# Second norm of a hybrid decoder layer: where the matmul with ones, the first silu and gate products, and three of the products x*r stand in the queues

## The chip, the cores and the metric

The kernel runs on one core of one Trainium2 chip. A core has four compute engines, each with its own queue of instructions in a fixed order: TensorE (PE in the profile; its weight loads are PEld), VectorE (DVE), ScalarE (ACT) and GpSimd (POOL). SyncE (SP) issues DMAs. An instruction starts when its engine has come to it and when what it waits for has been signalled, so an instruction that waits holds up all that is queued behind it on its engine. The metric is the device time of one execution in microseconds (us), as a median over runs.

## The reference

One layer of a decoder trunk for 512 prompt tokens and 8 sample tokens, all in fp32, with D = 1024 features. The change touches only the border between the attention/recurrent mix and the feed-forward network (FFN):

```python
x = x + g1 * mixed                       # mixed = (...) @ w_o
h2 = rms_norm(x, norm2_g) * (1.0 + sc2) + sh2
gu, up = jnp.split(h2 @ w_ffn_in, 2, axis=-1)      # 1024 -> 2 * 2816
x = x + g2 * ((jax.nn.silu(gu) * up) @ w_ffn_out)  # 2816 -> 1024
```

with `rms_norm(x, g) = x * rsqrt(mean(x*x) + eps) * g` over the features. `sc2`, `sh2` and the gates come from the conditioning and are one value per feature for the prompt, and one per feature and token for the samples. A final norm follows.

## The kernel before, in words

**Layout.** All activations are held transposed: features on the 128 partitions, tokens along the row. `x` is eight tiles of 128 features x 520 tokens (512 prompt tokens, then 8 sample columns). The 520 columns are worked in two halves of 260 (`HALVES`).

**Products.** Each fp32 operand is split in two numbers of a shorter format, a high part (`...h`, `whi`) and a rest (`...l`, `wlo`); a product is three matmuls (high x high, rest-weight x high, high x rest) for each of eight feature tiles, so a *half product* is 24 matmuls of 128x128 by 128x260 (`part_product`, L302 to L309). In each group of three the rest operand `h2l` is used last. Weight splits (a cast on ACT, a subtraction on DVE, L249 and L251) are made a few products ahead, into a ring of three buffers; raw weights come by DMA from SP's queue into a ring of two (`load_chunks`).

**The second norm.** `by_halves("wo", ...)` runs the products with `w_o`, first half of the tokens for all eight feature tiles, then the second half. After each one `residual` adds the result to `x` (DVE), and `sum_squares` squares it on ACT (L399) and adds it to `ss2` on POOL, or on DVE for the last two tiles (L400). `rstd_half` (L402) then sums over the partitions by a matmul with a 128x128 matrix of ones into the bank `r` (L407, plain fp32, two passes in the trace), takes the root on ACT (L408, one table load of its own) and the reciprocal on DVE (L409). `h2_half` (L1435) makes, for each feature tile f, the product x*r (L1446: POOL for the first half, DVE for the second), the high part `h2h` on ACT (L1448), the scaled and shifted value again on ACT or DVE (L1453, L1455), two small products for the 8 sample columns on POOL (L1450, L1451) with a copy of these 8 columns on ACT (L1457), and the rest `h2l` on DVE (L1458). The first half's norm is done inside the `w_o` products (`wo_between`).

**The first two FFN tiles.** The loop at L1640 runs four products (gate and up of two tiles of 128 hidden features) by halves: m = 0 to 3 for the first half of the tokens, then again for the second half. m even is a gate product, followed by `swish` (silu on ACT, L1500); m odd is an up product, followed by `times_up` (silu(gate) * up on DVE, L1504). Between the first half's m = 0 and m = 1 stands the second half's norm, as the second half's x is complete only when the last `w_o` product has been evacuated. Products from the second half need `h2h` and `h2l` of it. PSUM has 8 banks that are handed out in turn.

After that come the tiles 2 and 3 as whole products (`ffn_tile`; `fig`, `fiu` in the trace), and from tile 4 on `fast_tile`, which needs sums and differences of blocks of h2 that POOL makes (`h2_blocks`, L1577).

**What sets the order.** The order of each engine's queue is written at build time: a planner goes through the program with estimated times, takes for each engine what is ready by these estimates, and among ready work what stands first in the code. So the queues need not follow the code line by line. `tc.issue_after(ins)` keeps the instructions traced inside it behind `ins` in the queue of that instruction's engine; it adds no wait between engines.

Of the kernel before, what the change touches and what calls it, by code (L numbers as in the profile page):

```python
# [11 lines left out]
AF = mybir.ActivationFunctionType  # L12
ALU = mybir.AluOpType
# [4 lines left out]
D = 1024  # L18
# [10 lines left out]
HALF = NT // 2  # L29
HALVES = ((0, HALF), (HALF, NT))  # L30
# [35 lines left out]
def kernel(ctx, tc, xT, par, gates, b_f, cst, cse, own, cache_k, cache_v, cache_lf, pt,  # L66
# [3 lines left out]
    pe, act, dve, pool, sp = nc.tensor, nc.scalar, nc.vector, nc.gpsimd, nc.sync  # L70
# [9 lines left out]
    def slot(name, cols=NT, dt=F32, parts=128):  # L80
        return heap.tile([parts, cols], dt, name=name, tag="slot")

    def bank(name, parts=128, cols=512):
        return psp.tile([parts, cols], F32, name=name, tag="bank")
# [9 lines left out]
    x = []  # L94
# [12 lines left out]
    eps = keep.tile([128, 1], F32, name="eps")  # L107
# [76 lines left out]
    state = {"n": 0, "dma": 0, "split": 0, "load": 22, "lead": 11, "due": 0, "age": 1}  # L184
# [19 lines left out]
    def load_chunks(upto):  # L204
        while state["dma"] < len(chunks) and state["dma"] <= upto:
            c = state["dma"]
            if c in joined:
                raw = pgp.tile([128, GROUP, 256], F32, name="wraw", tag="pg")
            else:
                raw = wp.tile([128, KT, 256], F32, name="wraw", tag="wraw", bufs=2)  # L210
            o = 0
            for src, r0, nk, c0, n in chunks[c]:
                sp.dma_start(raw[:, :nk, o:o + n],
                             src[r0:r0 + nk * 128, c0:c0 + n].rearrange("(k p) c -> p k c", p=128))
                o += n
            raws[c] = raw
            state["dma"] += 1
# [70 lines left out]
    def begin(last=None):  # L288
        n = state["n"]
        state["n"] += 1  # L290
        last = len(units) - 1 if last is None else last
        if n < 42:
            tick(KEYS[n], n in VALUES)
        load_chunks(units[reach(n, last, state["load"])][0])
        split_upto(reach(n, last, state["lead"]))
        flush()
        return n

    def half_product(n, j, a, out):
        part_product(n, *HALVES[j], (lambda k: a(k, j)) if callable(a) else a, out)  # L300

    def part_product(n, t0, t1, a, out):  # L302
        hi, lo = splits[n]
        nk = units[n][2]
        for k in range(nk):
            ah, al = a(k) if callable(a) else (v[:, t0:t1] for v in a[k])
            for m, (wt, at) in enumerate(((hi, ah), (lo, ah), (hi, al))):
                state["mm"] = pe.matmul(out[:, :t1 - t0], lhsT=wt[k], rhs=at, start=k == 0 and m == 0,  # L308
                                        stop=k == nk - 1 and m == 2)  # L309

    def run_later(n):
        for fn in later.pop(n, []):
            fn()
# [88 lines left out]
    def rstd_half(name, ssum, r, j, more=()):  # L402
        t0, t1 = HALVES[j]
        ps = bank(f"{name}_{j}")
        parts = [ssum[:, t0:t1], *more]
        for n, q_ in enumerate(parts):
            pe.matmul(ps[:, :HALF], lhsT=ones, rhs=q_, start=n == 0, stop=n == len(parts) - 1)  # L407
        act.activation(r[:, t0:t1], ps[:, :HALF], AF.Sqrt, bias=eps, scale=1.0 / D)  # L408
        dve.reciprocal(r[:, t0:t1], r[:, t0:t1])  # L409

    def amplitude(name, scl, g):
# [125 lines left out]
    for f in range(KT):  # L537
        t = slot("sq1")
# [14 lines left out]
    for f in range(KT):  # L553
        t = slot("xn")
# [10 lines left out]
    for g3 in (0, 3):  # L565
# [10 lines left out]
        for n in range(6):  # L576
            t0, t1 = HALVES[n % 2]
# [317 lines left out]
    ready = []  # L895
    for i in range(KT):
        if i % 4 == 0:
            qtp.append(bank(f"qt{i}", NS))
        if i < 6:
            t = qpart[i]  # L900
            for j, (t0, t1) in enumerate(HALVES):
                b = bank(f"q{i}_{j}")
# [3 lines left out]
        else:  # L906
            t = slot("q")
# [521 lines left out]
    ss2, r2 = slot("ss2"), slot("r2")  # L1429
    h2 = []  # L1430
# [4 lines left out]
    def h2_half(j):  # L1435
        t0, t1 = HALVES[j]
        e_ = min(t1, NP)
        for f in range(KT):
            if j == 0:
                h2.append((slot("h2h", dt=F32R), slot("h2l", dt=F32R)))  # L1440
                if f % 2 == 0:
                    pair = pgp.tile([128, 2, NT], F32, name="h2r", tag="pg")
                    h2raw.extend((pair[:, 0], pair[:, 1]))
            t = h2raw[f]
            hi, lo = h2[f]
            (dve if j else pool).tensor_tensor(t[:, t0:t1], x[f][:, t0:t1], r2[:, t0:t1], ALU.mult)  # L1446
            a_, b_ = amp2[0][:, f], mod[:, 3, f]
            act.activation(hi[:, t0:e_], t[:, t0:e_], AF.Identity, scale=a_[:, 0:1], bias=b_[:, 0:1])  # L1448
            if j:
                pool.tensor_tensor(t[:, NP:], t[:, NP:], a_[:, 1:9], ALU.mult)  # L1450
                pool.tensor_tensor(t[:, NP:], t[:, NP:], b_[:, 1:9], ALU.add)  # L1451
            if j and f in ON_ACT:
                act.activation(t[:, t0:e_], t[:, t0:e_], AF.Identity, scale=a_[:, 0:1], bias=b_[:, 0:1])  # L1453
            else:
                dve.tensor_scalar(t[:, t0:e_], t[:, t0:e_], a_[:, 0:1], b_[:, 0:1], ALU.mult, ALU.add)  # L1455
            if j:
                act.copy(hi[:, NP:], t[:, NP:])  # L1457
            dve.tensor_tensor(lo[:, t0:t1], t[:, t0:t1], hi[:, t0:t1].bitcast(F32), ALU.subtract)  # L1458
# [32 lines left out]
    def wo_between(j):  # L1491
        rstd_half("r2", ss2, r2, j)
        h2_half(j)
# [12 lines left out]
    def last_product(ac):  # L1506
# [40 lines left out]
        for j, (t0, t1) in enumerate(LAST_PARTS):  # L1547
            for i in range(KT):
                if j == 0:
                    begin(u + KT - 1)  # L1550
                b = bank(f"fo{i}_{j}")
                part_product(u + i, t0, t1, ac, b)
                done(i, j, t0, t1, b)
                if j and i == 0:
                    norm(0, *LAST_PARTS[0])
        norm(1, *LAST_PARTS[1])

    def pair_out():
        return slot("ach", dt=F32R), slot("acl", dt=F32R)
# [78 lines left out]
    ac, ts, ready = [], [slot("sw") for _ in range(PLAIN)], []  # L1638
    u = state["n"]
    for j in range(2):  # L1640
        for m in range(2 * PLAIN):
            if j == 0:
                begin(u + 3)
            b = bank(f"fi{m}_{j}")
            half_product(u + m, j, h2, b)
            ready.append((times_up if m % 2 else swish, b, ts[m // 2], j))
            if j == 0 and m == 0:
                rstd_half("r2", ss2, r2, 1)
            if j or m:
                for fn, *args in ready:  # L1650
                    fn(*args)
                ready.clear()
            if j == 0 and m == 0:
                h2_half(1)
            first = u + 2 * PLAIN
            if j == 0:
                load_chunks(units[first + m][0])
            elif m:
                split_upto(first + m - 1)
    for t in ts:  # L1660
        out = pair_out()
# [72 lines left out]
```

## Time and profile before

| what | us |
|---|---|
| runs | 1032.33, 1027.59, 1031.36 |
| median | 1031.36 |
| the profiled execution | 1029.59 |
| its span (first to last instruction) | 1027.9 |
| PE busy | 992.3 (97%) |
| DVE busy | 796.8 (78%) |
| ACT busy | 551.0 (54%) |
| POOL busy | 328.6 (32%) |
| granted TensorE clock, mean | 0.994 |

The times of the trace are counted from the start of the span. In a timeline row stand the start, the duration, the engine, the line of the kernel, the operation, what it writes and reads, and in brackets how long the engine was idle before it and what ended that. Rows of several equal instructions are merged (x4). Matmuls overlap in the pipeline: each is shown with some 0.28 us while they start 0.12 us apart. A row of the waits reads: who waited, for whom, us in total, times, the longest. A row of groups with three numbers gives the shortest, median and longest duration in ns.

The part of the trace that matters runs from 658.8 us, the first FFN matmul, to 685.8 us, the first matmul of tile 2.

### The profile page before, as it was taken

To read this page: it belongs to the slowest core of one execution; us is meant where nothing else is said; L and a number is where in the kernel's file an instruction comes from. 1 tells how busy PE (TensorE), PEld (TensorE's weight loads), DVE (VectorE), ACT (ScalarE), POOL (GpSimd) and SP (SyncE) were. 2 spreads that over 40 slices of the span, in tenths; PEclk is the share of its full clock that TensorE was granted. 3 is DMA by queue.
4 is the path that set the end of the run, shared out by engine and by line. 5 is a ranking of instruction groups with operands and counts; after the bars stand their busy time and mean duration, and the time that the engine had idled before them with its cause. 6 is when DMAs were issued, how large, how long until landed. Compare 5 with 4: busy or idle time off the path is not lost.

```text
span 1027.9 us, 21296 instructions
## 1 busy us (share of the span) xinstructions
PE 992.3 (97%) x7994; PEld 918.8 (89%) x7994; DVE 796.8 (78%) x1423; ACT 551.0 (54%) x1132; POOL 328.6 (32%) x424
## 2 busy tenths in 40 slices
PE   4999999999999999999999999999999999999996
PEld 1788989999898988878888989999999999999996
DVE  5446999998989987886756544878888888888864
ACT  4433665857682267776875233565444444445453
POOL 0214511111133235654430001484432433434212
PEclk9899999999999999999999999999999999999998
DMA  9987987878888999988665784324243342333212
GB/s 323 307 280 285 306 290 217 261 233 276 261 254 310 323 314 306 310 259 274 219 235 185 252 302 126 83 62 115 71 124 99 87 124 72 93 104 103 62 63 84
DMA packets 165419, 206.99 MB, mean 201 GB/s; under 512 B 9906, under 2 KB 126146, under 8 KB 165250
## 3 DMA queue, kind: packets, MB, share of 16 engines
q1 hardware_dynamic: 148594, 152.52, 47.9%
q0 software_dynamic: 13040, 46.67, 13.7%
q10 hardware_dynamic: 3680, 6.42, 1.7%
q8 instruction: 63, 1.03, 0.4%
q14 instruction: 42, 0.34, 0.1%
HBM read 192.49 MB, written 13.09 MB: 200 GB/s over the span
## 4 chain that ended last, share of the span: by engine, by line
PE 70%; DVE 14%; DMA 6%; ACT 5%; issue 3%; SPq 0%; POOL 0%; POOLq 0%; DVEq 0%; ACTq 0%
PE fo L308 12%; PE pb L308 4%; PE gb L308 4%; PE ga L308 3%; PE k L308 3%; PE wo L308 3%; PE v L308 3%; DVE wlo L251 2%; DMA wraw<-in_w_in_dram 2%; PE gr L308 2%; PE xr L308 2%; DVE pg L733 2%; PE qp L530 2%; PE pv L818 2%; PE po L1261 2%
## 5 line engine op out<-in xcount | busy, mean ns | idle before, releaser
L249 ACT CAST whi<-wraw 128x1024 fp32r<-128x1024 f32 (+1 forms) x79 | 82.0, 1039 | 121.2 <-PE pb L308 35.1
L251 DVE TENSOR_TENSOR wlo<-wraw,whi 128x1024 fp32r<-128x1024 f32 (+1 forms) x79 | 101.3, 1284 | 32.6 <-ACT whi L249 30.5
L273 ACT CAST wb<-ws 128x512 fp32r<-128x512 f32 x72 | 44.8, 622 | 91.1 <-PE fo L308 63.6
L308 PE MATMUL fo<-ach,wb 128*128 128x260 f32 x512 | 93.3, 282 | 0.0
L685 POOL DMA_DIRECT2D pg<-in_cache_k_dram x74 | 39.4, 533 | 142.7 <-DVE S L734 70.3
L308 PEld LDWEIGHTS fo<-ach,wb 128*128 128x128 f32 x512 | 78.8, 188 | 0.0
L274 DVE TENSOR_TENSOR wb<-wraw,wb 128x512 fp32r<-128x512 f32 x86 | 74.2, 863 | 5.0 <-ACT wb L273 4.4
L274 DVE TENSOR_TENSOR wb<-ws,wb 128x512 fp32r<-128x512 f32 x72 | 65.8, 913 | 14.0 <-ACT wb L273 12.2
L264 POOL TENSOR_TENSOR ws<-wraw 128x512 f32<-128x512 f32 x18 | 26.6, 1480 | 153.8 <-DMA wraw<-in_w_fi_dram 124.8
L308 PE MATMUL fo<-acl,wb 128*128 128x260 f32 x256 | 72.3, 282 | 0.0
L273 ACT CAST wb<-wraw 128x512 fp32r<-128x512 f32 x86 | 53.6, 623 | 32.7 <-ACT cp L1622 5.8
L733 DVE TENSOR_TENSOR pg<-pg,qb 128x1024 f32<-128x1024 f32 x48 | 58.0, 1227 | 2.5 <-DMA pg<-in_cache_k_dram 2.4
L734 DVE TENSOR_REDUCE S<-pg 128x16 f32<-128x1024 f32 x48 | 57.0, 1207 | 0.1
L1218 POOL TENSOR_SCALAR p<-p,mu 128x128 f32<-128x128 f32 (+3 forms) x28 | 36.4, 1310 | 49.2 <-DVE mu L1214 31.3
L308 PEld LDWEIGHTS fo<-acl,wb 128*128 128x128 f32 x256 | 48.2, 188 | 0.0
L1212 ACT ACTIVATE p<-p,mu 128x128 f32<-128x128 f32 (+3 forms) x64 | 35.3, 553 | 15.9 <-DVE mu L1211 15.6
L308 PE MATMUL v<-hh,whi 128*128 128x260 f32 x128 | 37.3, 291 | 1.1 <-DVE pl L1232 1.1
L308 PE MATMUL pb<-oh,whi 128*128 128x260 f32 x128 | 36.7, 287 | 1.0 <-ACT oh L1319 1.0
L308 PE MATMUL k<-hh,whi 128*128 128x260 f32 x128 | 37.3, 291 | 0.0
L308 PE MATMUL gb<-hh,whi 128*128 128x260 f32 x128 | 37.0, 289 | 0.0
L308 PE MATMUL ga<-hh,wlo 128*128 128x260 f32 x128 | 36.3, 284 | 0.7 <-DVE wlo L251 0.7
L308 PE MATMUL pa<-gl,whi 128*128 128x260 f32 x128 | 36.1, 282 | 0.7 <-DVE gl L342 0.7
(1099 smaller groups left out, 3965.8 us busy)
## 6 DMA issues: line engine op xcount, KB each, us to landing
araw<-in_ada_w_dram SPq DMA_DIRECT2D x48, 512.0 KB, 7.0
wraw<-in_w_fi_dram SPq DMA_DIRECT2D x44, 512.0 KB, 4.7
pg<-in_cache_k_dram POOLq DMA_DIRECT2D x42, 512.0 KB, 6.0
pg<-in_cache_v_dram SPq DMA_DIRECT2D x42, 512.0 KB, 5.1
wraw<-in_w_in_dram SPq DMA_DIRECT2D x34, 512.0 KB, 7.8
wraw<-in_w_in_dram SPq DMA_DIRECT2D x11, 1024.0 KB, 10.0
pg<-in_cache_v_dram POOLq DMA_DIRECT2D x22, 512.0 KB, 6.4
pg<-in_cache_k_dram POOLq DMA_DIRECT2D x32, 256.0 KB, 5.7
```

What stands on the lines that cost most here:

```text
L249: state["act"] = act.copy(hi[:, :k1 - k0], src)
L251: state["last"] = dve.tensor_tensor(lo[:, :k1 - k0], src, hi[:, :k1 - k0].bitcast(F32), ALU.subtract)
L264: pool.tensor_tensor(s1, a21, a22, ALU.add)
L273: state["act"] = act.copy(t[:, :4], src)
L274: state["last"] = dve.tensor_tensor(t[:, 4:], src, t[:, :4].bitcast(F32), ALU.subtract)
L308: state["mm"] = pe.matmul(out[:, :t1 - t0], lhsT=wt[k], rhs=at, start=k == 0 and m == 0, stop=k == nk - 1 and m == 2)
L530: state["mm"] = pe.matmul(b[:, :HALF], lhsT=wt, rhs=at[:, t0:t1], start=k == 0 and m == 0, stop=k == 3 and m == 2)
L685: done.append(eng.dma_start(pg, cache[bass.ds(r, 1), :, c0:c1].rearrange("a p c -> (a p) c")))
L733: dve.tensor_tensor(pg, pg, q, ALU.mult)
L734: last = dve.tensor_reduce(S[r // 2][:, c:c + H], pg.rearrange("p (h d) -> p h d", d=DH), AX.X, ALU.add)
L1212: act.activation(p[:, :n + 128], p[:, :n + 128], AF.Exp, bias=mu[:, 0:1], scale=-1.0, accum_out=mu[:, 1:2])
L1218: (pool.tensor_scalar(p, p, mu[:, 2:3], None, ALU.mult) if a and i + 1 < KT else act.activation(p, p, AF.Copy, scale=mu[:, 2:3]))
```

## The change

Three edits:

1. The matmul with ones for the second half is issued inside the second half product (m = 1, first half of the tokens), after the fourth of its eight feature tiles, through a new argument `mid` of `half_product` and `part_product`. Before, it came after the product m = 0. `h2_half(1)` moves with it, behind the product m = 1.
2. `rstd_half` keeps its root instruction in `state["root"]`; what follows the products (`swish`, `times_up`) is traced inside `issue_after(root)`. The root is on ACT, so the silus are tied; a gate product reads a silu's output and so follows.
3. In the second half of `h2_half` the products x*r of the feature tiles 5, 6 and 7 go to POOL; tiles 0 to 4 stay on DVE.

The code order of `load_chunks` for the next chunk (m = 0) and of `begin` for m = 1 is thereby ahead of the norm's second half. No operation is added or dropped, no size is changed.

```diff
-    def half_product(n, j, a, out):
-        part_product(n, *HALVES[j], (lambda k: a(k, j)) if callable(a) else a, out)
+    def half_product(n, j, a, out, mid=None):
+        part_product(n, *HALVES[j], (lambda k: a(k, j)) if callable(a) else a, out, mid)
 
-    def part_product(n, t0, t1, a, out):
+    def part_product(n, t0, t1, a, out, mid=None):
...
                 state["mm"] = pe.matmul(out[:, :t1 - t0], lhsT=wt[k], rhs=at, start=k == 0 and m == 0,
                                         stop=k == nk - 1 and m == 2)
+            if mid is not None and k == nk // 2 - 1:
+                mid()
...
-        act.activation(r[:, t0:t1], ps[:, :HALF], AF.Sqrt, bias=eps, scale=1.0 / D)
+        state["root"] = act.activation(r[:, t0:t1], ps[:, :HALF], AF.Sqrt, bias=eps, scale=1.0 / D)
         dve.reciprocal(r[:, t0:t1], r[:, t0:t1])
...
-            (dve if j else pool).tensor_tensor(t[:, t0:t1], x[f][:, t0:t1], r2[:, t0:t1], ALU.mult)
+            (dve if j and f < 5 else pool).tensor_tensor(t[:, t0:t1], x[f][:, t0:t1], r2[:, t0:t1], ALU.mult)
...
             b = bank(f"fi{m}_{j}")
-            half_product(u + m, j, h2, b)
+            half_product(u + m, j, h2, b, (lambda: rstd_half("r2", ss2, r2, 1)) if j == 0 and m == 1 else None)
             ready.append((times_up if m % 2 else swish, b, ts[m // 2], j))
-            if j == 0 and m == 0:
-                rstd_half("r2", ss2, r2, 1)
+            if j == 0 and m == 1:
+                h2_half(1)
             if j or m:
-                for fn, *args in ready:
-                    fn(*args)
+                with tc.issue_after(state["root"].ins):
+                    for fn, *args in ready:
+                        fn(*args)
                 ready.clear()
-            if j == 0 and m == 0:
-                h2_half(1)
```

## The prediction

> **What bounds the kernel now.** I read the page first, for the span and the busy shares, then the windows by stage, then TensorE's waits on either side of the change, and at last the order of each engine's instructions in that stage. From the page:
>
> ```profile
> span 1027.9 us, 21296 instructions
> ...
> PE 992.3 (97%) x7994; PEld 918.8 (89%) x7994; DVE 796.8 (78%) x1423; ACT 551.0 (54%) x1132; POOL 328.6 (32%) x424
> ...
> L249 ACT CAST whi<-wraw 128x1024 fp32r<-128x1024 f32 (+1 forms) x79 | 82.0, 1039 | 121.2 <-PE pb L308 35.1
> L251 DVE TENSOR_TENSOR wlo<-wraw,whi 128x1024 fp32r<-128x1024 f32 (+1 forms) x79 | 101.3, 1284 | 32.6 <-ACT whi L249 30.5
> ```
>
> TensorE (PE) is busy 97% of the span, but that is a mean. The windows below are the eight half products of the first two FFN tiles (the stage that is changed), and all from there to the final norm. Columns: window, length, then busy time of PE, weight loads, DVE, ACT, POOL.
>
> ```profile
> 658.79:685.78 26.99, 24.49 (x196) 23.63 (x195) 18.83 (x36) 16.92 (x34) 16.59 (x29) 1.00 0.15 41
> 685.78:1003.00 317.22, 317.22 (x2639) 316.98 (x2638) 260.76 (x492) 151.54 (x314) 118.95 (x81) 1.00 0.34 96
> ```
>
> The changed stage has 26.99 - 24.49 = 2.5 us in which PE is idle; the 317.22 us behind it have none, at full clock (1.00). So time won in the stage moves all that follows forward, and it can win little more than those 2.5 us. TensorE's waits in the stage:
>
> ```profile
> PEld fi L308 <- DVE h2l L1458: 1.7, 3, 0.7
> PE r L407 <- DVE ss L400: 1.4, 1, 1.4
> PE fi L308 <- DVE h2l L1458: 1.1, 3, 0.4
> ```
>
> Two stalls are there to be had: 1.4 us where the matmul with ones (r, L407) waits for the last sum of squares, and 1.1 us (matmuls) to 1.7 us (their weight loads) where the first products of the second half wait for their rest operands h2l. I take 1.6 for the second, near the weight-load row, since a matmul can't start ahead of its weights.
>
> **The matmul with ones, moved.** It now stands behind the 24 matmuls of the first half product; it goes behind the first 12 of the second one. PE's order around it:
>
> ```profile
> 661.54 0.28 PE L308 MATMUL fi<-h2l,whi 128*128 128x260 f32 x1
> 663.22 0.68 PE L407 MATMUL r<-ss,cs 128*128 128x260 f32 x2 [1.40 <-DVE ss L400]
> ...
> 663.85 0.28 PE L308 MATMUL fi<-h2h,wlo 128*128 128x260 f32 x1
> ...
> 672.37 0.28 PE L308 MATMUL fi<-h2h,whi 128*128 128x260 f32 x1
> ```
>
> A half product is 24 matmuls and takes 2.88 us (the first one begins the window, at 658.79, and its last matmul starts at 661.54: 23 steps, 0.12 each). Twelve are 1.44 us, so PE comes to r at 661.66 + 1.44 = 663.10, and its sum is there when it is today, for 663.22. The wait shrinks from 1.4 to about 0.1, and PE is 1.4 us ahead when it goes on. If the build put r in another place this would fall to zero; nothing makes it a loss. The second half's first product then begins at 672.37 - 1.44 = 670.93. No DMA moves with r, and the weight load that the code now issues ahead of it is on SP's queue, behind nothing here.
>
> **The root and the reciprocal.** ACT and DVE, in order:
>
> ```profile
> 662.63 1.28 ACT L1500 ACT_TABLE_LOAD   x1
> 663.92 0.39 ACT L1500 ACTIVATE sw<-fi 128x260 f32<-128x260 f32 x1
> 664.33 1.28 ACT L408 ACT_TABLE_LOAD   x1
> 665.62 0.48 ACT L408 ACTIVATE r<-r,eps 128x260 f32<-128x260 f32 x1
> 669.48 0.60 ACT L1448 ACTIVATE h2h<-h2r,mod,n2amp 128x252 fp32r<-128x252 f32 x1 [3.38 <-DVE h2r L1446]
> ...
> 676.10 1.28 ACT L1500 ACT_TABLE_LOAD   x1
> ...
> 677.68 0.59 ACT L1453 ACTIVATE h2r<-h2r,mod,n2amp 128x252 f32<-128x252 f32 x1
> ```
> ```profile
> 666.87 0.43 DVE L1504 TENSOR_TENSOR sw<-fi,sw 128x260 f32<-128x260 f32 x1 [3.80 <-PE fi L308]
> 667.22 1.77 DVE L409 RECIPROCAL r<-r 128x260 f32<-128x260 f32 x1
> 669.01 1.46 DVE L1446 TENSOR_TENSOR h2r<-x,r 128x260 f32<-128x260 f32 x4
> ...
> 678.37 0.67 DVE L1458 TENSOR_TENSOR h2l<-h2r,h2h 128x260 fp32r<-128x260 f32 x1
> ```
>
> In the code the root stands ahead of the first silu; in the queues it is the other way round. So ACT loads the silu table (1.28), does silu, loads the root's table (1.28) and is done with the root at 666.10; and the reciprocal, queued on DVE behind the gate product that waits 3.80 for PE, starts only at 667.22. The tie takes both away. ACT is free at 662.63: root table to 663.91, r ends at 663.90, root from 663.95 to 664.43, reciprocal (1.77) from 664.47 to 666.24. The products x*r begin at 666.24 in place of 669.01: 2.8 us earlier.
>
> Does that load wait for its operand? For the final norm it didn't:
>
> ```profile
> 1002.31 1.28 ACT L1537 ACT_TABLE_LOAD   x1
> 1002.43 0.64 PE L1536 MATMUL r<-ss,cs 128*128 128x280 f32 x2
> ```
>
> The load starts ahead of the matmul that feeds the root. I take it so; if it waited, the root would come 1.3 us later.
>
> What waits behind the tied silu: its table load and itself, 1.28 + 0.39 = 1.67 from 664.43 to 666.10, lie under the reciprocal, and ACT's first scaled copy would come at 666.24 + 0.47 = 666.71. It costs nothing; without that cover the 1.67 would stand ahead of the whole second half. The later switch at 676.10 goes, as the silu table stays loaded, so the last feature's copy (677.68) loses 1.58 in front of it. The gate product falls among DVE's x*r work, 0.43; its bank is needed again only by the eighth bank from there, many microseconds later.
>
> [...]
>
> **Three products x*r on POOL.** DVE loses three of eight, 3 x 0.37 (1.46 for four) = 1.1 us. POOL takes them on in front of or between its small products for the eight sample columns:
>
> ```profile
> 643.61 8.38 POOL L1446 TENSOR_TENSOR h2r<-x,r 128x260 f32<-128x260 f32 x8 [12.31 <-DVE rs L1424]
> ```
> ```profile
> 669.52 0.32 POOL L1450 TENSOR_TENSOR h2r<-h2r,n2amp 128x8 f32<-128x8 f32 x1 [9.64 <-DVE h2r L1446]
> ...
> 674.57 0.27 POOL L1451 TENSOR_TENSOR h2r<-h2r,mod 128x8 f32<-128x8 f32 x1
> ```
>
> ```profile
> L1458 DVE TENSOR_TENSOR h2l<-h2r,h2h x16: 417/428/969, 646.3 to 678.4; 128x260 fp32r<-128x260 f32 x16
> ...
> L1446 POOL TENSOR_TENSOR h2r<-x,r x8: 747/878/1809, 643.6 to 651.2; 128x260 f32<-128x260 f32 x8
> ```
>
> (The last two rows are groups: ns of the shortest, the median and the longest.) The first half's eight products on POOL took 8.38, 1.05 each beside a busy DVE. Three are 3.1 us. The eight small pairs run from 669.52 to 674.84, 5.3 us. POOL therefore has 8.4 us where it had 5.3, and is done at 666.24 + 8.4 = 674.7. ACT's work is 676.10 - 669.48 = 6.6 plus the fourth copy 0.6 and a silu 0.4: from 666.71 to 674.3. So POOL is late next: the last feature needs its small pair, then a copy of eight columns and the subtraction, some 0.6 more: 675.3. PE in strict order wants it at 670.93 + 23 x 0.12 = 673.7: 1.6 late. Today the last h2l is done at 679.04 where strict order wants it at 672.37 + 2.76 = 675.13, 3.9 late, and PE pays only 1.6 (41%), since matmuls of the next product are queued ahead of the late ones. At the same rate 1.6 late costs 0.65; ends are 0 (h2l in time) and 1.6 (nothing queued ahead). I take 0.65.
>
> Against the move: half of the h2l subtractions on DVE take up to 0.43, the longest 0.97, and the last one (678.37), which runs after POOL has gone on from the small pairs to larger work, 0.67. If each POOL product holds a DVE subtraction by the whole 0.5 between them, that is 1.5 lost for 1.1 won. [...]
>
> **The sum.** 1.4 (r) + 1.6 (today's h2l stall) - 0.65 (what is left) = 2.4 us, with ends 1.4 and 3.0. Behind the stage nothing takes it back as the rows stand: PE has no idle time from 685.78 on. The profiled execution took 1029.59 (span 1027.9), 1.8 under the median 1031.36 of the runs shown; it would become about 1027.2, and the median about 1029.0. A measurement of this kernel tells about 0.5%, 5 us, from no change: the forecast lies within.
>
> **The rivals.**
> - *Only r's stall goes.* The late operands hang on POOL's queue as much as they did on ACT's, and the h2l stall stays at 1.6 or near. Speaks for it: POOL's 8.4 us. Against: 2.8 us of earlier start. Gain 0.5 to 1.4, time 1030.2.
> - *POOL's products set the stage (slower).* Place: the last feature's x*r on POOL. At the longest single product of the first half, 1.81 each, and queued between the small pairs, POOL ends at 666.24 + 5.4 + 5.3 = 677.0, the last h2l at 677.6, 3.9 late again; with nothing queued ahead on PE all 3.9 count against the 3.0 saved: 0.9 slower, 1032.3. It decides from 3.0 us of lateness, an h2l at 676.7.
> - *The FFN's order is rewritten.* The queues' order behind the stage is decided at build time from estimated times, which shift. If weight splits then come late for PE, each costs at most a cast and a subtraction, 1.04 + 1.28 = 2.3 us; it is slower by over 0.5% from four of them on (2.4 won, 9.2 lost), 1038. For it: DVE has 260.76 of 317.22 us busy, the least room. Against: PE waits nowhere there now.
> - *The tie or r's place doesn't take in the queues* (silu still first): no change beyond the POOL move, 1031.4.
>
> **How the numbers follow.** Forecast (1.4 to 3.0 gained) 0.62; only r 0.15; POOL slower 0.08; order rewritten 0.09; no effect 0.06. The forecast's own range is 1028.4 to 1030.0; three runs lie 4.7 us apart, so a median may stand 1.5 to 2 off, 1026.5 to 1032. The other cases but the rewritten order reach to 1032.3, with the same scatter 1033.5. I give 1026 to 1033.5. Beyond 0.5%: slower is the rewritten order, 0.09; faster needs 5.2 us where the stage has 3.0 to give, so only scatter or a luckier order, 0.05; the rest, 0.86, is within.
>
> **What would show it.** Right: r's wait on PE near 0.1; ACT's order root, silu, with one load before each and none near 676; reciprocal at about 664.5; x*r at 666.2; h2l waits on PE under 1; the tile behind (fig) starting near 683.4 in place of 685.78. Wrong: a reciprocal still behind the gate product; POOL's last small pair past 676; new PE waits on wlo or wb behind 686.

## The result: slower by 0.3%

| | median, us | runs |
|---|---|---|
| before | 1032.8 (1027.59 to 1036.63) | 22 |
| changed | 1036.04 (1032.10 to 1039.21) | 22 |
| ratio | 1.0031, 95% interval 1.0018 to 1.0044 | |

The change costs 1.9 to 4.5 us where 2.4 us of gain was forecast, and the median lies above the range. The profiled execution took 1035.54 (span 1033.9).

"Stage" below means the time from the first FFN matmul to the first one of tile 2 (`fig`). It is 26.99 us before; in the changed kernel (first row; the second row is the 317.22 us behind it, the third a part of the stage; columns as in the prediction, the granted TensorE clock third from the end):

```profile
662.83:691.83 29.00, 26.70 (x197) 25.33 (x196) 21.36 (x34) 14.48 (x32) 21.08 (x35) 0.94 0.20 57
691.83:1009.05 317.22, 317.22 (x2640) 316.97 (x2639) 255.70 (x491) 152.48 (x314) 112.01 (x78) 1.00 0.33 94
677.80:681.20 3.40, 3.40 (x14) 3.17 (x15) 3.36 (x6) 3.16 (x11) 2.63 (x4) 0.51 0.01 2
```

The stage is 2.0 us longer. Behind it nothing changed: PE is busy for all of 317.22 us, as before. Ahead of it the queues hold the same instructions in the same order; the stage starts 4.0 us later in this execution, but that start lies anywhere between 658.2 and 664.1 us in the fourteen executions traced for this study, so it isn't the change. The third row is the surprise: for 3.4 us TensorE ran at half its clock.

What PE waited for in the changed stage, and one wait of ACT:

```profile
PEld fi L308 <- DVE h2l L1460: 3.3, 5, 1.8
PE fi L308 <- DVE h2l L1460: 2.3, 2, 1.6
ACT h2h L1459 <- POOL h2r L1453: 2.5, 1, 2.5
```

The 1.4 us for r are gone, as forecast. The wait for h2l has doubled (2.3 in place of 1.1, 3.3 in place of 1.7 by the weight loads). The order of ACT, DVE and POOL shows why:

```profile
667.97 0.48 ACT L410 ACTIVATE r<-r,eps 128x260 f32<-128x260 f32 x1 [1.32 <-PE r L409]
668.47 1.28 ACT L1502 ACT_TABLE_LOAD   x1
669.76 0.39 ACT L1502 ACTIVATE sw<-fi 128x260 f32<-128x260 f32 x1
671.12 1.09 ACT L1450 ACTIVATE h2h<-h2r,mod,n2amp 128x252 fp32r<-128x252 f32 x2 [0.97 <-POOL h2r L1448]
674.73 0.20 ACT L1459 CAST h2h<-h2r 128x8 fp32r<-128x8 f32 x1 [2.53 <-POOL h2r L1453]
...
676.09 0.58 ACT L1455 ACTIVATE h2r<-h2r,mod,n2amp 128x252 f32<-128x252 f32 x1
```
```profile
668.48 1.78 DVE L411 RECIPROCAL r<-r 128x260 f32<-128x260 f32 x1 [1.37 <-ACT r L410]
670.18 0.43 DVE L1506 TENSOR_TENSOR sw<-fi,sw 128x260 f32<-128x260 f32 x1
670.53 2.96 DVE L1448 TENSOR_TENSOR h2r<-x,r 128x260 f32<-128x260 f32 x4
...
674.97 0.43 DVE L1460 TENSOR_TENSOR h2l<-h2r,h2h 128x260 fp32r<-128x260 f32 x1 [0.80 <-ACT h2h L1459]
...
676.77 1.30 DVE L1460 TENSOR_TENSOR h2l<-h2r,h2h 128x260 fp32r<-128x260 f32 x2
...
678.43 2.21 DVE L1460 TENSOR_TENSOR h2l<-h2r,h2h 128x260 fp32r<-128x260 f32 x3
...
681.49 0.77 DVE L1460 TENSOR_TENSOR h2l<-h2r,h2h 128x260 fp32r<-128x260 f32 x1
...
682.52 0.63 DVE L1460 TENSOR_TENSOR h2l<-h2r,h2h 128x260 fp32r<-128x260 f32 x1
```
```profile
670.34 1.63 POOL L1448 TENSOR_TENSOR h2r<-x,r 128x260 f32<-128x260 f32 x2 [6.42 <-DVE r L411]
671.94 0.39 POOL L1452 TENSOR_TENSOR h2r<-h2r,n2amp 128x8 f32<-128x8 f32 x1
672.28 0.92 POOL L1448 TENSOR_TENSOR h2r<-x,r 128x260 f32<-128x260 f32 x1
673.17 0.39 POOL L1453 TENSOR_TENSOR h2r<-h2r,mod 128x8 f32<-128x8 f32 x1
673.52 0.86 POOL L1452 TENSOR_TENSOR h2r<-h2r,n2amp 128x8 f32<-128x8 f32 x3
674.35 0.51 POOL L1453 TENSOR_TENSOR h2r<-h2r,mod 128x8 f32<-128x8 f32 x3
...
676.72 0.73 POOL L1582 TENSOR_TENSOR u<-h2r 128x260 f32<-128x260 f32 x1
```

Two things happen at once. On POOL the three products, and small products of other features, stand ahead of feature 0's own small product: its last step is in the row at 674.35, and ACT waits 2.53 us for it (674.73). And DVE's four products take 2.96 us in place of 1.46: beside POOL's products three of them take 0.84 to 0.97 us each in place of 0.42 or 0.43, one still 0.42. So x*r starts 7.7 us into the stage in place of 10.2, but the first h2l is written 12.6 us into the stage, where it was 12.7 before. All that the earlier start won is lost before the first operand is out.

PE comes to the second half 1.4 us earlier (674.99). It takes the first h2l with hardly a wait (675.45); what it waits 1.55 us for is the second. Feature 1's scaled value stands on ACT behind what feature 0 held up (676.09), and its subtraction on DVE (676.77) takes 0.96 us in place of 0.42, as POOL has gone on to the first block sum (676.72). Of the six subtractions behind it, four are slowed in the same way, to between 0.63 and 0.97 us. The last h2l is written at 683.15:

```profile
667.26 0.68 PE L409 MATMUL r<-ss,cs 128*128 128x260 f32 x2
...
674.99 0.39 PE L308 MATMUL fi<-h2h,whi 128*128 128x260 f32 x1
...
675.45 0.38 PE L308 MATMUL fi<-h2l,whi 128*128 128x260 f32 x1
...
677.79 0.53 PE L308 MATMUL fi<-h2l,whi 128*128 128x260 f32 x1 [1.55 <-DVE h2l L1460]
678.12 0.42 PE L308 MATMUL fi<-h2h,whi 128*128 128x260 f32 x1
678.34 0.42 PE L308 MATMUL fi<-h2h,wlo 128*128 128x260 f32 x1
...
682.31 0.39 PE L308 MATMUL fi<-h2l,whi 128*128 128x260 f32 x1 [0.73 <-DVE h2l L1460]
...
683.20 0.51 PE L308 MATMUL fi<-h2l,whi 128*128 128x260 f32 x2
```

Behind the 1.55 us the matmuls start 0.22 us apart in place of 0.12: the half clock. But the clock is back at 1.00 when PE waits again, 0.73 us for the h2l before the last (682.31), and at 683.20 it takes the last one 0.05 us after it is written. So late operands, and not the clock, decide when PE gets past this point; from there on it runs at full pace.

Where the 2.0 us lie can be read from the last h2l. It is written 20.3 us into the stage, and before it was as late (678.37 + 0.67 = 679.04, 20.3 us into the stage). But then PE didn't wait for it, as it had other matmuls ahead of those that need it, and only 6.7 us of its work in the stage were left. Now 8.7 us are left: PE has done 2.0 us less by then.

### The profile page after: what moved, and what is told of

It reads as the page before. It is cut to its first block, busy times and chain, and to the rows that moved or that the text cites. A ratio compares the mean times of both kernels' runs of the same rounds, so it can differ in the third digit from the quotient of the medians.

```text
span 1033.9 us, 21290 instructions
## 1 busy us (share of the span) xinstructions
PE 996.5 (96%) x7994; PEld 922.3 (89%) x7994; DVE 793.2 (77%) x1420; ACT 549.7 (53%) x1130; POOL 326.9 (32%) x427
## 4 chain that ended last, share of the span: by engine, by line
PE 78%; DVE 7%; DMA 6%; ACT 4%; issue 3%; POOL 1%; SPq 0%; POOLq 0%; DVEq 0%; ACTq 0%
PE fo L308 12%; PE wo L308 5%; PE pb L308 4%; PE gb L308 4%; PE v L308 4%; PE k L308 4%; DMA wraw<-in_w_in_dram 3%; PE ga L308 3%; PE gr L308 2%; PE xr L308 2%; PE pv L820 2%; PE po L1263 2%; PE qp L532 2%; PE q L532 1%; PE fi L308 1%
## 5 line engine op out<-in xcount | busy, mean ns | idle before, releaser
L251 DVE TENSOR_TENSOR wlo<-wraw,whi 128x1024 fp32r<-128x1024 f32 (+1 forms) x79 | 97.4, 1232 | 35.7 <-ACT whi L249 33.7
L274 DVE TENSOR_TENSOR wb<-ws,wb 128x512 fp32r<-128x512 f32 x72 | 65.2, 906 | 16.1 <-ACT wb L273 14.3
L264 POOL TENSOR_TENSOR ws<-wraw 128x512 f32<-128x512 f32 x18 | 24.1, 1341 | 160.4 <-DMA wraw<-in_w_fi_dram 121.4
L308 PE MATMUL ga<-hh,whi 128*128 128x260 f32 x128 | 37.1, 290 | 0.0
L308 PE MATMUL v<-hl,whi 128*128 128x260 f32 x128 | 37.1, 290 | 0.0
```

The costliest lines, as they stand in the source:

```text
L251: state["last"] = dve.tensor_tensor(lo[:, :k1 - k0], src, hi[:, :k1 - k0].bitcast(F32), ALU.subtract)
L264: pool.tensor_tensor(s1, a21, a22, ALU.add)
L274: state["last"] = dve.tensor_tensor(t[:, 4:], src, t[:, :4].bitcast(F32), ALU.subtract)
```

## The experiments

Three theories. *POOL*: the three products moved there do the harm, by POOL's queue (1a) or by a conflict with DVE's instructions (1b; the expectations name it "port", but the runs show only that DVE's instructions take longer beside POOL's, not what in the chip slows them). *Order* (2): the tie and r's new place bring PE earlier to operands that come no earlier. *Clock* (3): a part of the loss isn't the stall but the half clock behind it.

All results in one table, from one profiled execution each; waits are the sums of PE's rows in the stage for r, h2l and h2h (in brackets those of its weight loads for h2l and h2h), an h2l is given by the end of its subtraction, counted from the stage's start, and times go against the kernel before on the same chip.

| kernel | stage, us | waits, us | half clock, us | first h2l, us | last h2l, us | ratio (95% interval) |
|---|---|---|---|---|---|---|
| before | 26.99 | 1.4 + 1.1 (1.7) | 0 | 12.7 | 20.3 | |
| changed | 29.00 | 2.3 (3.3) | 3.4 | 12.6 | 20.3 | 1.0031 (1.0018 to 1.0044) |
| e1_no_pool | 25.4 | 1.2 (1.6) | 0 | 10.2 | 17.0 | 0.9981 (0.9964 to 0.9999) |
| e2_pool_only | 30.3 | 1.4 + 2.1 (3.4) | 3.4 | 14.7 | 22.9 | 1.0027 (1.0012 to 1.0041) |
| e3_r_only | 25.9 | 1.2 (2.0) | 0 | 11.6 | 19.2 | 0.9993 (0.9977 to 1.0010) |
| e4_tie_only | 25.8 | 1.4 + 0.3 (0.5) | 0 | 10.0 | 16.8 | 0.9996 (0.9981 to 1.0011) |
| e5_pairs_dve | 30.7 | 2.5 (3.9) | 6.8 | 11.7 | 20.0 | 1.0030 (1.0014 to 1.0046) |
| e6_pool_late | 30.5 | 2.5 (4.0) | 6.8 | 10.7 | 19.9 | 1.0024 (1.0011 to 1.0037) |
| e7_fill | 30.8 | 1.5 (2.5) | 3.4 | 12.6 | 20.3 | 1.0036 (1.0022 to 1.0049) |
| e8_hold_sums | 24.4 | 0.3 (0.5) | 0 | 10.2 | 16.1 | 0.9969 (0.9956 to 0.9982) |
| e10_before_hold | 25.8 | 1.4 + 0.4 (0.6) | 0 | 12.7 | 20.0 | 1.0005 (0.9988 to 1.0021) |
| e11_after_hold | 27.9 | 1.7 (2.3) | 3.4 | 12.6 | 18.6 | 0.9992 (0.9977 to 1.0007) |
| e12_fill48 | 29.4 | 0 | 0 | 12.5 | 20.4 | 1.0027 (1.0010 to 1.0045) |

A sum accounts for the stages: 192 matmuls x 0.12 = 23.0, r itself 0.5, the wait for r, the weight loads' wait for operands, and half of the time at half clock. It gives 28.5 for the changed kernel (29.0 measured), 30.0 for e2_pool_only (30.3), 25.1 for e1_no_pool (25.4) and 24.0 for e8_hold_sums (24.4). It says where PE's time went, not what each part would give back: time lost to the half clock isn't won at full clock if the next operand is late anyway.

**Nothing moved to POOL; r's place and the tie kept.**

```diff
-            (dve if j and f < 5 else pool).tensor_tensor(t[:, t0:t1], x[f][:, t0:t1], r2[:, t0:t1], ALU.mult)
+            (dve if j else pool).tensor_tensor(t[:, t0:t1], x[f][:, t0:t1], r2[:, t0:t1], ALU.mult)
```

> The changed kernel with all eight products x*r of the second half on DVE again; r's place and the tie are kept. Stage = from the first FFN matmul to the first one of tile 2: 26.99 us before, 29.00 after. Theory 1 (POOL): the three products on POOL hold up DVE's own products and the small sample products, and with them the first h2l; without them x*r starts at the same early place (7.7 us into the stage), the four first DVE products take 1.5 us in place of 2.96, the first h2l is done some 2 us earlier, and the stage takes 24.5 to 26.0 us: 1 to 2.5 us faster than before. Theory 2 (order): PE comes 1.4 us earlier to operands that the tie and the new queue order don't bring earlier; the stage stays at 28 us or more.

The stage takes 25.4 us, 1.6 less than before, and the kernel is faster than before by a hair. This decides between POOL and order: the same tie and the same r, without POOL's part, gain. DVE's products and the two slowest subtractions, and what PE still waits for:

```profile
670.48 1.45 DVE L1448 TENSOR_TENSOR h2r<-x,r 128x260 f32<-128x260 f32 x4
...
677.07 1.84 DVE L1460 TENSOR_TENSOR h2l<-h2r,h2h 128x260 fp32r<-128x260 f32 x2
```
```profile
678.08 0.39 PE L308 MATMUL fi<-h2l,whi 128*128 128x260 f32 x1 [0.96 <-DVE h2l L1460]
```

**The POOL move alone, on the kernel before.** The diff is the inverse of the one above.

> The kernel before with the three products x*r on POOL as the only change. Theory 1 (POOL): the four DVE products at the head take near 3 us in place of 1.46 and the first small sample product ends some 3 us after the reciprocal; stage 28.5 to 31 us, slower than before by 1.5 to 4 us. Theory 2 (order): POOL's part is harmless, stage 26.5 to 27.5.

Stage 30.3 us, 0.27% slower than before: POOL's part alone makes more than the whole loss of the changed kernel (3.3 of 2.0 us in the stage); the other two parts take some of it back.

**Only r moved.** No tie, all products on DVE:

```diff
-                with tc.issue_after(state["root"].ins):
-                    for fn, *args in ready:
-                        fn(*args)
+                for fn, *args in ready:
+                    fn(*args)
```

> The kernel before with only the matmul with ones moved (no tie, all products on DVE). Both theories: r's wait on PE near 0.1 in place of 1.4. If the late h2l alone sets the second half, the 1.4 us come back as a longer wait for h2l: stage 26 to 27 us, no gain over 1 us. If silu and the gate product still stand ahead of the reciprocal, x*r starts only 0 to 1.5 us earlier than before.

Stage 25.9, just under what was expected; x*r starts 9.2 us into the stage, 1.1 earlier than before. r's 1.4 us are not all given back.

**Only the tie**, on the kernel before:

```diff
-        act.activation(r[:, t0:t1], ps[:, :HALF], AF.Sqrt, bias=eps, scale=1.0 / D)
+        state["root"] = act.activation(r[:, t0:t1], ps[:, :HALF], AF.Sqrt, bias=eps, scale=1.0 / D)
...
-                for fn, *args in ready:
-                    fn(*args)
+                with tc.issue_after(state["root"].ins):
+                    for fn, *args in ready:
+                        fn(*args)
```

> The kernel before with only the tie of the silus behind the root (r stays between the two products, all products on DVE). x*r then starts 2.5 to 2.8 us earlier, as in the changed kernel; r's wait stays at 1.4. Theory 1: the stall for h2l goes from 1.1 to under 0.5 and the stage is 25 to 26 us. Theory 2 (the tie harms): stage 27 us or more.

Stage 25.8: x*r starts 2.7 us earlier and the wait for h2l falls to 0.3. The order theory falls: neither part harms. For e3_r_only and e4_tie_only the gain of some 1 us is within what the timing can tell.

**Queue or conflict: the small products on DVE.** POOL keeps the three x*r alone:

```diff
-                pool.tensor_tensor(t[:, NP:], t[:, NP:], a_[:, 1:9], ALU.mult)
-                pool.tensor_tensor(t[:, NP:], t[:, NP:], b_[:, 1:9], ALU.add)
+                dve.tensor_tensor(t[:, NP:], t[:, NP:], a_[:, 1:9], ALU.mult)
+                dve.tensor_tensor(t[:, NP:], t[:, NP:], b_[:, 1:9], ALU.add)
```

> The changed kernel with the sixteen small products for the sample columns on DVE in place of POOL, so that the three products x*r are alone on POOL. Stage: 26.99 us before, 29.00 after, 25.4 with nothing moved to POOL. Theory 1a (queue): what hurt was that the first feature's small product stood on POOL behind the three x*r; the first h2l then comes 10 to 11 us into the stage (12.6 in the changed kernel) and the stage takes 25.5 to 27 us. Theory 1b (port): what hurt is that DVE's two-input instructions run at half pace beside POOL's; the four first products on DVE still take near 3 us, the first h2l comes at 11.5 or later and the stage takes 27.5 us or more.

Without the queue on POOL the first h2l comes only 0.9 us earlier, the last 0.3, and the stage takes 30.7 us. As 1b had it; but DVE has sixteen more instructions here, so this run alone doesn't separate the two. And a part of its stage is the clock: at half rate well past the last h2l, the 72 matmuls left need 10.3 us, where 72 x 0.12 are 8.6 (an estimate, as the one for the next run).

**The products behind the first two small products on POOL.**

```diff
-            (dve if j and f < 5 else pool).tensor_tensor(t[:, t0:t1], x[f][:, t0:t1], r2[:, t0:t1], ALU.mult)
+            with tc.issue_after(state["pair"].ins) if j and f >= 5 else nullcontext():
+                (dve if j and f < 5 else pool).tensor_tensor(t[:, t0:t1], x[f][:, t0:t1], r2[:, t0:t1], ALU.mult)
...
-                pool.tensor_tensor(t[:, NP:], t[:, NP:], b_[:, 1:9], ALU.add)
+                p_ = pool.tensor_tensor(t[:, NP:], t[:, NP:], b_[:, 1:9], ALU.add)
+                if f < 2:
+                    state["pair"] = p_
```

> The changed kernel with the three products x*r on POOL queued behind the small products of the features 0 and 1. Theory 1a (queue): the first h2l is as early as with nothing on POOL (10.2 us into the stage), stage 25 to 26.5 us. Theory 1b (port): the three products take as much from DVE wherever they stand: the first h2l is early, but the later ones are held, stage 26.5 to 28.5 us, and no gain over the kernel with nothing on POOL.

The head is nearly as early as without POOL (10.7), DVE's four products take 1.45 again, and still the stage is 30.5, beyond what either side expected; 1.5 of it is the half clock, as above (10.1 in place of 8.6). The same two effects now hit feature 2. DVE's first subtraction beside the products, ACT's wait for the third small product, and POOL:

```profile
668.90 0.97 DVE L1463 TENSOR_TENSOR h2l<-h2r,h2h 128x260 fp32r<-128x260 f32 x1
```
```profile
671.94 0.20 ACT L1462 CAST h2h<-h2r 128x8 fp32r<-128x8 f32 x1 [2.02 <-POOL h2r L1454]
```
```profile
668.66 1.82 POOL L1449 TENSOR_TENSOR h2r<-x,r 128x260 f32<-128x260 f32 x2
```

So it is both, queue and conflict, in both places tried; how the loss divides between the two is left open.

**The clock: more work in front of the stall.** 24 matmuls more between the token halves, into a bank that nobody reads:

```diff
+            if j == 0 and m == 3:
+                half_product(u + m, 0, h2, bank("fill"))
```

> The changed kernel with 24 matmuls added (the last half product of the first token half once more, into a bank that nobody reads) between the first and the second token half: 2.9 us more work for TensorE just where it is about to stall. Theory 3 (clock): a part of the loss is the TensorE clock, granted at half for some 3.4 us after the stall; without the stall it stays at 1.00 and the stage takes 27 to 28.5 us, less than the 29.00 of the changed kernel although there is more work. Against it: if the stall alone cost the time, the added work takes its place at best, stage 29.2 us or more.

The stage takes 30.8 us, more than either side expected. The 2.9 us of work left a wait of 1.5 us in three pieces (0.26, 0.99, 0.27), and the half clock came all the same, here behind the last h2l, where PE waits for nothing more: 73 matmuls take 10.4 us in place of 8.8. It tells nothing against the clock theory, but the filling was too small to test it. So twice the filling, two half products in the same place:

> The changed kernel with 48 added matmuls (5.8 us of work) between the token halves: enough that TensorE comes to the second half after the late h2l are there. Theory 3 (clock falls because of the stall): no stall over 0.5 us, clock 1.00 in the stage, stage = 23.0 + 0.5 + 5.8 = 29.3 us, no longer than the changed kernel's 29.00 by more than 0.5 although it has 5.8 us more work (24 added matmuls took 30.75 and left a stall of 1.5 us with the half clock). If the half clock comes from something else in this stage, it comes again: 31 us.

Stage 29.4 us, no wait and the clock at 1.00 throughout: the half clock comes with the stall, not with what else happens in this stage. The run also tells what the half clock cost the changed kernel. At full clock the last h2l is written 20.4 us into the stage, no earlier than the 20.3 there, where PE takes it at once and has 8.6 us of matmuls left: 29.0, the changed kernel's stage. By these rows the changed kernel lost nothing to its half clock; at full clock PE would have waited longer for the same operands. And 48 matmuls, 5.75 us of work that nobody needs, cost only 0.4 us because they fill that wait.

**What a stall costs.** In the fastest kernel (below), eight stalls of growing length in front of FFN tiles, made by a matmul that waits for a chain of small copies on ACT:

```diff
+    GAPS = {5: 1, 7: 3, 9: 5, 11: 7, 13: 9, 15: 11, 17: 13, 19: 16}
+
+    def gap(n):
+        b = bank("gap")[:, :HALF]
+        hh = h2[0][0]
+        with tc.issue_after(state["mm"].ins):
+            pe.matmul(b, lhsT=hh[:, :128], rhs=hh[:, :HALF], start=True, stop=True)
+        t_ = sm.tile([128, 64], F32R, name="gapt", tag="s_gap", bufs=1)
+        act.copy(t_, b[:, :64])
+        for _ in range(n - 1):
+            act.copy(t_, t_.bitcast(F32))
+        return pe.matmul(b[:, :64], lhsT=hh[:, :128], rhs=t_, start=True, stop=True)
...
+        with tc.issue_after(gap(GAPS[jt]).ins) if jt in GAPS else nullcontext():
```

> The fastest kernel so far (block sums held back, nothing moved to POOL) with eight stalls of TensorE of growing length put in front of the FFN tiles 5, 7, ... 19: a matmul that waits for a chain of 1, 3, 5, 7, 9, 11, 13 and 16 small copies on ACT, some 0.8 to 4.5 us, with 30 us of dense matmuls between. It tells what a stall costs beside its own length. Theory 3 (clock): up to a stall of about 1 to 1.5 us the granted clock stays at 1.00; behind the longer ones it is 0.50 for some 3.4 us, which costs 1.7 us each; the time behind the stage grows by the sum of the stalls (about 20 us) and 1.7 us for each stall that trips the clock (4 to 7 of them). Against it: the clock stays at 1.00 behind all, and the time grows by the stalls alone.

Two runs, 1076.59 and 1072.08 us. The stalls came out longer than planned, 1.1 to 7.1 us, 29.75 in all. Three of them, and the clock behind the second and the third (windows of 1 us each):

```profile
728.65 0.30 PE L1676 MATMUL gap<-gapt,h2h 128*128 128x64 f32 x1 [1.12 <-ACT gapt L1673]
...
762.33 0.30 PE L1676 MATMUL gap<-gapt,h2h 128*128 128x64 f32 x1 [1.58 <-ACT gapt L1675]
...
797.17 0.30 PE L1676 MATMUL gap<-gapt,h2h 128*128 128x64 f32 x1 [2.76 <-ACT gapt L1675]
```
```profile
763.33:764.33 1.00, 1.00 (x10) 1.00 (x10) 0.43 (x1) 0.19 (x2) 0.00 (x0) 1.00 0.00 0
798.17:799.17 1.00, 1.00 (x6) 1.00 (x6) 0.00 (x0) 0.00 (x0) 0.00 (x0) 0.50 0.00 0
801.17:802.17 1.00, 1.00 (x10) 1.00 (x10) 0.14 (x2) 0.18 (x1) 0.00 (x0) 0.95 0.00 0
```

Behind 1.12 and 1.58 us the clock stays at 1.00. Behind 2.76 us it is 0.50, and in the window that begins 4 us behind the stall 0.95 again; the half clock lasts about 3.4 us. The stalls of 3.53, 4.18 and 4.56 us each bring about 3.4 us of half clock; behind 4.94 it is about 6.0 and behind 7.08 about 4.0, and in both it sets in before the stall ends. So half clock comes with six of the eight. Here PE is the limit on both sides of a stall, and one of these six costs its own length plus half of the 3.4 us at 0.50, 1.7 us, or more (an estimate from these rows). The sum bears this out: from the first `fig` matmul to the end it takes 386.45 us where e8_hold_sums takes 342.05. Of these 44.4 us the stalls are 29.75 and half of the half clock behind them 11.9; 2.8 are left for the sixteen added matmuls.

A stall's length alone doesn't tell whether half clock follows: in the changed kernel it follows 1.55 us (677.79 above), though 1.58 us did nothing here. In the changed kernel's trace half clock comes three times between 30 us and the end of the stage, at 281.93, 387.74 and 677.88 us, and lasts 3.41 us each time. Two stretches of this length, one that ends where the third begins and holds the 1.55 us, and one that holds the 1.58 us:

```profile
674.47:677.88 3.41, 1.86 (x12) 1.33 (x10) 1.96 (x4) 3.10 (x10) 2.67 (x12) 1.00 0.01 2
```
```profile
760.31:763.72 3.41, 1.83 (x15) 1.62 (x14) 2.97 (x6) 2.23 (x7) 0.82 (x1) 1.00 0.01 2
```

Of the 12 matmuls that PE works on in the first, 10 start in it, of the 15 in the second 13; at full pace it is 28. Behind the first the clock is 0.50, behind the second 1.00. Short waits that came together were followed by it too: in e7_fill the 3.41 us ahead of the half clock hold 0.26 + 0.99 + 0.27 and 10 starts, while behind the 0.96 and 0.26 of e1_no_pool, 1.2 in all, the clock stays at 1.00. What decides between 1.55 and 1.58 us these runs don't show.

**The conflict again: the block sums held back.** In e1_no_pool two h2l subtractions took 1.84 us, 0.92 each, at 677.07, while POOL had gone on from its small products to the sums and differences of h2 blocks (`h2_blocks`) that a later tile needs. All products stay on DVE, as in e1_no_pool, and the sums wait for the last h2l:

```diff
-            for k in range(4):
-                h2_blocks(k)
+            gate_ = small("hold", 128, 1)
+            held_ = pool.tensor_copy(gate_, h2[KT - 1][1][:, NT - 1:NT].bitcast(F32))
+            with tc.issue_after(held_.ins):
+                for k in range(4):
+                    h2_blocks(k)
```

> All eight products on DVE (as in the run without POOL's products), and POOL's block sums of h2 held back until the last h2l is written. In the run without POOL's products the last three h2l took 0.92, 0.92 and 0.62 us beside the block sums, and TensorE stalled 1.2 us for them. Theory 1b (port): they take 0.42 each now, the stall falls under 0.5, and the stage takes 24.2 to 25 us in place of 25.4. Theory 1a (queue only): no effect on the stage, 25.4. Risk in both: the sums come 2.5 us later on POOL; if the blocks are then late for tile 4, the time behind the stage grows over the 342.1 us of all runs so far.

DVE's last subtractions, and the first sum on POOL behind them:

```profile
673.48 0.77 DVE L1460 TENSOR_TENSOR h2l<-h2r,h2h 128x260 fp32r<-128x260 f32 x2
...
674.93 0.43 DVE L1460 TENSOR_TENSOR h2l<-h2r,h2h 128x260 fp32r<-128x260 f32 x1
```
```profile
675.42 0.19 POOL L1668 COPY hold<-h2l 128x1 f32<-128x1 f32 x1 [2.62 <-DVE h2l L1460]
675.56 0.74 POOL L1582 TENSOR_TENSOR u<-h2r 128x260 f32<-128x260 f32 x1
```

With POOL quiet the subtractions take 0.42 or 0.43 each (two in 0.77 where they overlap), the wait on PE falls from 1.2 to 0.3, and the stage to 24.4 us. The conflict (1b) is thereby shown on instructions whose place in the queue nobody touched. This is the fastest version: 1028.36 us (1027.38 to 1029.2), 0.31% under the kernel before, [0.9956, 0.9982], and ahead of the changed one.

**The same hold on the kernel before.**

> The kernel before with POOL's block sums held back until the last h2l is written, as the only change. In the kernel before the second-half subtractions beside the sums took 0.92 us and TensorE waited 1.1 to 1.7 us for h2l, but part of that is the switch to the silu table in front of the last feature. Theory 1b (port): 0.5 to 1 us of the stage go (26 to 26.5 us); the switch stays, so not more. Without a port effect: 27.0.

Stage 25.8, the wait for h2l 0.4 in place of 1.1: in the stage it works. But no time is won over the runs (1.0005), and the 317.20 us behind the stage show PE idle for 0.86 of them, which neither the kernel before nor e8_hold_sums does:

```profile
686.40:1003.60 317.20, 316.34 (x2626) 315.58 (x2625) 263.01 (x490) 150.25 (x311) 124.97 (x87) 1.00 0.33 96
```
```profile
PE fo L308 <- DVE wb L274: 0.4, 1, 0.4
PE fi4x L1613 <- DVE wb L274: 0.3, 1, 0.3
PE fo L308 <- DVE acl L1463: 0.2, 1, 0.2
```

From the first `fig` matmul to the end it takes 343.9 us, where the kernel before takes 342.2. PE now waits for operands that DVE makes for later tiles; that they are late because of the held sums is the likely reading and wasn't tried further, and 0.8 of the 1.7 us isn't accounted for by these waits. In e8_hold_sums, where the last h2l comes earlier in the stage (16.1 us in place of 20.0), the same stretch takes 342.0.

**The same hold on the changed kernel.**

> The changed kernel (three products on POOL) with POOL's block sums held back until the last h2l is written. If the products themselves do the harm, the first h2l stays at 12.6 us into the stage, TensorE still stalls 2 us or more for it, and the stage is 27 to 29 us, with or without the half clock. If the products only pushed the block sums against the subtractions, the stage falls to 25.5 us or less.

The first h2l comes as late as without the hold (12.6 us into the stage), the last 1.7 us earlier (18.6), the stage is 27.9, and the clock is halved. So holding the sums back saves 1.1 of the changed kernel's 29.0 us. With them out of the way what remains is the harm of the three products themselves: 3.5 us against e8_hold_sums, which differs from it in nothing else.

## Why the prediction was wrong

**The matmul with ones: right.** r waits for nothing on PE and the second half's first products come 1.4 us earlier, as worked out.

**The root and the reciprocal: right, but for details.** One silu load is hidden under the reciprocal (668.47 and 668.48, both ending by 670.3), and the switch near 676 is gone. The load that I put in front of the root isn't there either: ACT's last table load ahead of this root (1.28 at 643.93) is the one for the first half's root, and no silu comes between. x*r starts 7.7 us into the stage where 7.45 was worked out: the gate product (0.43) went ahead of it.

**Three products on POOL: the step that failed.** I asked when POOL would be *done* and put the last h2l at 675.3, 16.5 us into the stage; it was written 20.3 us into the stage. POOL was done with the small products 13.9 us into the stage, earlier than my 15.9. But ACT and DVE work through the features in order, and I never worked out when feature 0's small product comes: it stands behind all three new products, ACT waits 2.53 us for it, and every feature behind it moves with it. Then the subtractions, which I took at their usual 0.42, ran beside POOL's block sums: with the sums held back the last h2l comes at 18.6, and without the three products on POOL as well at 16.1, close to the forecast. The claim that DVE loses 1.1 us of work fell with it: five products on DVE became four beside POOL at 0.74 each and one at 0.42, 3.4 us where the eight before took 3.2 (1.46 for four, 0.42 or 0.43 for the others). The longer DVE times beside POOL (0.97 against 0.43), a reason against the move in the prediction, should have been applied to x*r itself, and to the subtractions beside the block sums, where I left them out of the sum. So the start that the root gained, 2.5 us, was lost before the first operand. The term "0.65 left of the h2l stall" measured 2.3 by the matmuls and 3.3 by their weight loads.

**What the prediction has no term for: the clock.** The rows of before show no half clock in this stage, and I priced a stall at its length. The changed kernel has 3.4 us at 0.51, 1.7 us of PE's time. They look like the loss and aren't: the operand behind them came later still, as the rows at 682.31 and 683.20 and e12_fill48 show. They would have counted where PE is the limit behind a stall.

**The rivals.** "POOL's products set the stage" had the right engine, the right sign and a last h2l that PE waits for; it looked for the cause in the last feature's x*r on POOL, which was done 10.4 us into the stage, where it was feature 0's small product, and priced it at 0.9 against 2.0. "The FFN's order is rewritten" fell: the 317.22 us behind are 317.22 busy. "Only r's stall goes" and "doesn't take" fell too.

**What stays open.** How the harm of the three products (3.5 us with the sums held back) divides between POOL's queue and the conflict with x*r: the runs that move one also move the other. And the runs show +3.2 us where the profiled stage has +2.0; 1.2 lies within the interval (1.9 to 4.5). The mean granted clock doesn't explain them: it is 0.9900 over the changed kernel's 22 runs and 0.9918 over the 87 runs of before beside the experiments, but 3.4 us at half clock, as the changed stage has them, lower it by 0.0017 by themselves.

## What to carry to other kernels

When work goes to an engine with slack, work out when the *first* result comes out of each queue that the bottleneck engine reads from, not only when the last one does, as everything behind it in order moves with it. When elementwise work goes from VectorE to GpSimd, look at what VectorE does beside it: here three of four products beside GpSimd's took 0.84 to 0.97 us in place of 0.42 or 0.43, and VectorE's x*r took 3.4 us for five where it had taken 3.2 for eight. And price a half clock only where TensorE is the limit behind it: 3.4 us of it were worth 1.7 us beside the stall's own length in e9_gaps (half of them, at a clock of 0.50), and nothing in the changed kernel. So look whether the next operand would have let TensorE go on sooner.

## What the runs showed of the hardware that was not expected

- **Half clock behind a stall.** In the changed kernel 1.55 us was followed by 3.41 us at 0.50. Of the eight single stalls of e9_gaps, the six from 2.76 us on came with some 3.4 us of it or more; behind 1.12 and 1.58 us the clock stayed at 1.00.
- **A half clock can be free.** The changed kernel's 3.4 us ended before PE's next late operand; 3.4 us behind the last operand, in e7_fill, cost some 1.6.
- **DVE beside POOL.** x*r on DVE went from 0.42 or 0.43 to between 0.84 and 0.97 us, h2l from 0.42 to between 0.92 and 0.97; on POOL x*r took 0.74 to 0.94.
- **Unneeded work can be cheap.** 48 matmuls nobody reads, 5.75 us of them, cost the stage 0.4 us, because they stood where PE would have waited.
- **Slower runs had the lower mean clock.** For the kernel before, the median was 1035.4 us in runs with a mean granted clock under 0.9895 (6 runs), 1032.5 between 0.9895 and 0.9915 (28), 1031.7 up to 0.9935 (42) and 1029.8 above that (11).
